# The scan's decay exponents: one GpSimd addition over four heads in place of four ScalarE activations with bias

## The chip, the core and the metric

The kernel runs on one core of a Trainium2 chip. The metric is the device time of one execution in microseconds (us), lower is better. The engines of the core are called as in the profile: PE is TensorE (matmuls; PEld its weight loads), DVE is VectorE, ACT is ScalarE, POOL is GpSimd, and SP is SyncE, which issues nearly all DMAs.

## The reference, cut to what matters

The reference is one layer of a bidirectional hybrid encoder: RMS norm, one input projection, three parallel groups (a chunked state-space scan, a windowed attention, an attention over a memory), gates, and an output projection with a residual. There are ten tiles of 128 tokens: eight of the sample, two of the prompt. The change lies in the scan, of which this is the part that counts:

```
acs = jnp.cumsum(dt * A.astype(f32).reshape(g, r), axis=2)
xdt = xs * dt[..., None]
seg = acs[:, :, :, None] - acs[:, :, None, :]
decay = jnp.exp(jnp.where(tril, seg, -jnp.inf))
cb = jnp.einsum('bcign,bcjgn->bcijg', Cm, Bm)
y_diag = jnp.einsum('bcijgr,bcjgrp->bcigrp', cb[..., None] * decay, xdt)
```

A chunk is a tile of 128 tokens, there are 16 heads and two directions. For each tile, direction and head the kernel needs a 128x128 matrix of exponents: the cumulated decay of position i (along a row) plus a value that belongs to position j (one per partition: the logarithm of the step less the cumulated decay).

## The kernel before, in words

TensorE works on large projections in blocks. A block streams weights of 128x512 from HBM (L209, L271: four buffers), splits each into a rounded part (ACT, L202) and the rest (DVE, L203), three buffers each, and multiplies the activations with both (L254 to L256 where tokens are the output's rows, L289 to L291 where features are). At the beginning and at the end, blocks in seven products are used (L1199 to L1201); there POOL makes sums of weights (L1171).

Beside the projections of the middle part run small generators: attention (`attn`, L583), memory attention (`mem_attn`, L704), preparation of keys (`k_prep`, L476), the scan upward (`ssd_up`, L798) and downward (`ssd_down`, L998). Each generator does a little and yields. Two lanes hold the queues of generators, and after each step of a block `pump` (L155) lets the lanes go on by rates that are written out by hand (RATES, L32). The framework then orders the instructions of each engine from this sequence, from priorities, and from what it reckons to be ready. Every engine and the SP queue work in their order: what waits holds up what stands behind it.

`ssd_up` treats a tile of 128 tokens in four quarters of four heads. For a quarter q:

- `rows(q)` (L836) loads two tiles of 128x512, rf for the forward and rb (called mt in the code) for the backward direction: for each of four heads 128 cumulated decays, the same on all partitions. rf has two buffers, rb three. So the load of a late quarter waits until an earlier quarter's tile has been read: rf by the selection (L919), rb by the products of `diag` (L931).
- `expo(q)` (L908) adds to each group of 128 columns the value of its head, one per partition, from `wj_all` (a column of it per head).
- `choose(q)` (L916) selects on DVE between the two directions by the triangle (L919) and takes the exponential on ACT (L920), in place in rb.
- `weights(q)` (L922) multiplies by the product of C and B on DVE (L924).
- `diag(g)` (L927) multiplies with the inputs of eight heads on TensorE (L931, into py) and adds the result up on DVE (L937).

At L940 to L974 these stand in this order: `expo(0)`, three yields, `choose(0)`, `expo(1)`, `rows(2)`, three yields, `weights(0)`, `choose(1)`, a yield, `expo(2)`, a yield, `weights(1)`, a yield, `diag(0)`, `choose(2)`, `rows(3)`, three yields, `weights(2)`, a yield, `expo(3)`, two yields, `choose(3)`, a yield, `weights(3)`, two yields, `diag(1)`.

POOL has little to do in this part: `rsqrt` (L119) computes one over a root for attention (qr), keys (krr), memory attention (mr) and the scan downward (yrs) in two instructions (L120, L121), and DVE uses the result (L604, L488, L742, L984).

`hv(r, 4)` sees 512 columns as four times 128; `hb(a, 4, P)` spreads four columns so that each stands for 128.

Of the kernel before, what the change touches and what calls it, by code (L numbers as in the profile page):

```python
# [15 lines left out]
AF = mybir.ActivationFunctionType  # L16
ALU = mybir.AluOpType
AX = mybir.AxisListType

P = 128  # L20
# [23 lines left out]
def hymba_encoder_kernel(  # L44
# [7 lines left out]
    V, A, G, T, S = nc.vector, nc.scalar, nc.gpsimd, nc.tensor, nc.sync  # L52
# [26 lines left out]
    def lconst(shape, name, dtype=F32):  # L79
        return cl.tile(shape, dtype, tag=name, name=name)  # L80
# [42 lines left out]
    def hv(ap, n=8):  # L123
        return ap.rearrange("p (h d) -> p h d", h=n)

    def hb(ap, n, d):
        return ap.unsqueeze(2).broadcast_to([P, n, d])
# [670 lines left out]
    def ssd_up(t):  # L798
# [30 lines left out]
        for g in range(2):  # L829
            c = slice(8 * g, 8 * g + 8)  # L830
            V.scalar_tensor_tensor(out=dco[:, c], in0=dt_all[:, t, 16 + 8 * g:24 + 8 * g], scalar=cbd[:, g:g + 1],
                                   in1=dskip[:, c], op0=ALU.mult, op1=ALU.add)
# [29 lines left out]
        for g in range(2):  # L862
            c = slice(g * 512, (g + 1) * 512)
# [44 lines left out]
        def expo(q):  # L908

            for d, r in enumerate(rows_[q]):  # L910
                for j in range(4):
                    c = slice(j * P, (j + 1) * P)
                    h = 16 * d + 4 * q + j
                    A.activation(r[:, c], r[:, c], AF.Identity, bias=wj_all[:, (t + 1) % 6, h:h + 1])

        def choose(q):  # L916

# [9 lines left out]
        def diag(g):  # L927
# [10 lines left out]
            S.dma_start(yp_d[t][:, g * 512:(g + 1) * 512], ya[g])  # L938

        expo(0)  # L940
        yield
        yield
        yield
        choose(0)
        expo(1)
        rows(2)
        yield
# [3 lines left out]
        choose(1)  # L951
        yield
        expo(2)
        yield
        weights(1)
# [557 lines left out]
    wj_all = lconst([P, 6, 32], "wj_all")  # L1513
# [167 lines left out]
```

## Time and profile before

| what | value |
|---|---|
| median of 3 runs | 1804.47 us (1803.84 to 1804.49) |
| span of the profiled execution, first to last instruction | 1800.7 us |
| median of the runs less this span | 3.77 us |
| instructions | 30423 |
| granted TensorE clock, mean | 1.000 |
| `expo` on ACT | 320 activations of 128x128, from 492.5 to 1452.6 us |
| selection on DVE (L919) | 40 of 128x512, 742 ns each |
| exponential on ACT (L920) | 40 of 128x512, 630 ns each |
| POOL additions of 128x128 (L1171) | 4 x 144, in the first and the last part only |

Of the profiled execution only the span is given, so times are set against it and the 3.77 us are carried along. The profile has a page (busy time of each engine, the chain of work that ended last, the costliest groups of instructions) and answers to questions: groups of instructions by line, who waited for whom, busy time in chosen stretches, the chain, and single instructions in order of time. A row such as `L914 ACT ACTIVATE rf<-rf,wj_all 128x128 f32<-128x128 f32 x160` names line, engine, operation, tiles and shape written and read, and the count. Durations of matmuls overlap and their ends are modelled.

### The profile page before, as it was taken

How to read it: one execution, taken by the hardware profiler on the slowest of the kernel's cores; microseconds unless marked ns; L12 is line 12 of the kernel's file. 1: busy time of each engine (PE TensorE's matmuls, PEld its weight loads, DVE VectorE, ACT ScalarE, POOL GpSimd, SP SyncE). 2: the span in 40 equal slices, each digit the busy share in tenths (PEclk: the TensorE clock that was granted, in tenths of full speed). 3: DMA queues.
4: the chain of work that ended last, by engine and by line, in shares of the span. 5: the costliest groups of instructions: out<-in, count | busy, mean ns of one | idle time of the engine just before them, and what ended most of it. 6: DMA issues, size and time to landing. Idle time of an engine off the chain costs nothing.

```text
span 1800.7 us, 30423 instructions
## 1 busy us (share of the span) xinstructions
PE 1791.2 (99%) x10546; PEld 1606.1 (89%) x10546; DVE 1244.3 (69%) x2422; ACT 903.0 (50%) x2039; POOL 439.5 (24%) x714
## 2 busy tenths in 40 slices
PE   9999999999999999999999999999999999999999
PEld 7789999999887899999989987887898888889999
DVE  5595788877657978775755866666885654866665
ACT  6554455444445756564435646544574533543332
POOL 0105789961110000000000000001100000058775
PEclk9999999999999999999999999999999999999999
DMA  8664455446544644444436355457785564644442
GB/s 291 198 179 120 138 153 146 129 136 218 164 136 147 184 134 140 121 132 134 119 96 192 110 161 180 128 178 235 231 266 168 184 190 138 216 153 147 142 143 80
DMA packets 198891, 290.58 MB, mean 161 GB/s; under 512 B 18960, under 2 KB 80464, under 8 KB 198736
## 3 DMA queue, kind: packets, MB, share of 16 engines
q1 hardware_dynamic: 198592, 288.57, 52.7%
q8 instruction: 83, 1.36, 0.3%
q14 instruction: 72, 0.59, 0.1%
q10 hardware_dynamic: 144, 0.06, 0.0%
HBM read 231.12 MB, written 57.44 MB: 160 GB/s over the span
## 4 chain that ended last, share of the span: by engine, by line
PE 61%; DVE 1%; ACT 1%; issue 1%; DMA 1%; POOL 0%; POOLq 0%; ACTq 0%; DVEq 0%
PE acc L254 9%; PE acc L256 8%; PE acc L255 8%; PE acc L289 5%; PE acc L291 5%; PE acc L290 5%; PE acc L1199 3%; PE acc L1201 3%; PE acc L1200 3%; PE py L931 2%; PE po L674 1%; PE ppt L664 1%; PE accm L1200 1%; PE accm L1201 1%; PE accm L1199 1%
## 5 line engine op out<-in xcount | busy, mean ns | idle before, releaser
L203 DVE TENSOR_TENSOR wl<-wraw,wh 128x512 fp32r<-128x512 f32 (+1 forms) x480 | 338.9, 708 | 241.3 <-ACT wh L202 230.7
L254 PE MATMUL acc<-wh,xH 128*128 128x512 f32 (+1 forms) x1248 | 481.9, 386 | 0.2 <-ACT mkr L416 0.2
L255 PE MATMUL acc<-wl,xH 128*128 128x512 f32 (+1 forms) x1248 | 472.2, 378 | 0.9 <-DVE wl L203 0.6
L256 PE MATMUL acc<-wh,xL 128*128 128x512 f32 (+1 forms) x1248 | 472.8, 379 | 0.0
L202 ACT ACTIVATE wh<-wraw 128x512 fp32r<-128x512 f32 (+1 forms) x480 | 292.4, 613 | 323.5 <-PE acc L256 173.3
L254 PEld LDWEIGHTS acc<-wh,xH 128*128 128x128 f32 x1248 | 234.5, 188 | 45.1 <-issue 4.8
L255 PEld LDWEIGHTS acc<-wl,xH 128*128 128x128 f32 x1248 | 234.7, 188 | 43.8 <-DVE wl L203 3.3
L256 PEld LDWEIGHTS acc<-wh,xL 128*128 128x128 f32 x1248 | 234.2, 188 | 43.9 <-issue 0.9
L289 PE MATMUL acc<-xH,wh 128*128 128x320 f32 x640 | 204.5, 320 | 0.0
L291 PE MATMUL acc<-xH,wl 128*128 128x320 f32 x640 | 198.6, 310 | 0.0
L290 PE MATMUL acc<-xL,wh 128*128 128x320 f32 x640 | 198.3, 310 | 0.0
L203 DVE TENSOR_TENSOR sl<-ws,sh 128x384 fp32r<-128x384 f32 x144 | 99.6, 695 | 96.9 <-ACT sh L202 96.6
L202 ACT ACTIVATE sh<-ws 128x384 fp32r<-128x384 f32 x144 | 74.6, 523 | 176.5 <-POOL ws L1171 81.5
L1171 POOL TENSOR_TENSOR ws<-wraw 128x128 f32<-128x128 f32 x144 | 91.1, 633 | 202.0 <-DMA wraw<-in_w_in_pairs_dram 83.6
L289 PEld LDWEIGHTS acc<-xH,wh 128*128 128x128 f32 x640 | 120.3, 188 | 4.1 <-issue 3.7
L290 PEld LDWEIGHTS acc<-xL,wh 128*128 128x128 f32 x640 | 120.3, 188 | 2.6 <-issue 2.2
L291 PEld LDWEIGHTS acc<-xH,wl 128*128 128x128 f32 x640 | 120.1, 188 | 0.7 <-issue 0.6
L1171 POOL TENSOR_TENSOR ws<-wraw,ws 128x128 f32<-128x128 f32 x144 | 93.5, 649 | 11.3
L358 DVE SCALAR_TENSOR_TENSOR c<-u,vec,c 128x638 f32<-128x638 f32 (+1 forms) x96 | 88.6, 926 | 10.0 <-ACT c L353 9.7
L1171 POOL TENSOR_TENSOR ws<-ws,wraw 128x128 f32<-128x128 f32 x144 | 94.2, 654 | 0.0
L120 POOL TENSOR_SCALAR qr<-qss 128x8 f32<-128x8 f32 x10 | 4.3, 428 | 366.6 <-DVE qss L598 366.6
L1171 POOL TENSOR_TENSOR wraw<-wraw 128x128 f32<-128x128 f32 x144 | 89.2, 620 | 11.1
(427 smaller groups left out, 3645.1 us busy)
## 6 DMA issues: line engine op xcount, KB each, us to landing
wraw<-in_w_in_laid_dram SPq DMA_DIRECT2D x208, 256.0 KB, 2.8
wraw<-in_w_in_pairs_dram SPq DMA_DIRECT2D x80, 256.0 KB, 2.8
wraw<-in_w_out_laid_dram SPq DMA_DIRECT2D x64, 256.0 KB, 3.5
wraw<-in_w_out_pairs_dram SPq DMA_DIRECT2D x64, 256.0 KB, 2.8
rf<-ac SPq DMA_DIRECT2D x40, 256.0 KB, 3.7
rb<-ac SPq DMA_DIRECT2D x40, 256.0 KB, 4.1
wraw<-in_w_mem_laid_dram SPq DMA_DIRECT2D x32, 256.0 KB, 4.8
xst<-in_x_sample_dram SPq DMA_DIRECT2D x20, 256.0 KB, 4.7
```

The costliest lines, as they stand in the source:

```text
L202: a = A.activation(h, raw, AF.Copy)
L203: b = V.tensor_sub(l, raw, h.bitcast(F32))
L254: T.matmul(ps[t][:, :n], sh, h[:, :n], start=(k_ == 0), stop=False)
L255: T.matmul(ps[t][:, :n], sh, l[:, :n], start=False, stop=False)
L256: T.matmul(ps[t][:, :n], sl, h[:, :n], start=False, stop=(k_ == KT - 1))
L289: T.matmul(o, sh, cur["H", q][:, m, c], start=(k == 0), stop=False)
L290: T.matmul(o, sh, cur["L", q][:, m, c], start=False, stop=False)
L291: T.matmul(o, sl, cur["H", q][:, m, c], start=False, stop=(k == KT - 1))
L358: V.scalar_tensor_tensor(out=c[0], in0=u[:, k:k + n], scalar=cw[k], in1=c[0], op0=ALU.mult, op1=ALU.add)
L1171: G.tensor_tensor(out=o, in0=x, in1=y, op=op)
L1199: T.matmul(ps[p], h, xh, start=(k_ == 0), stop=False)
L1200: T.matmul(ps[p], h, xl, start=False, stop=False)
```

## The change

In `expo`, the four activations per direction, each with 128 columns and a bias of one value per partition, become one addition on POOL over 512 columns, whose second operand is four columns of `wj_all`, each spread over 128.

```diff
         def expo(q):
 
             for d, r in enumerate(rows_[q]):
-                for j in range(4):
-                    c = slice(j * P, (j + 1) * P)
-                    h = 16 * d + 4 * q + j
-                    A.activation(r[:, c], r[:, c], AF.Identity, bias=wj_all[:, (t + 1) % 6, h:h + 1])
+                h = 16 * d + 4 * q
+                G.tensor_tensor(out=hv(r, 4), in0=hv(r, 4), in1=hb(wj_all[:, (t + 1) % 6, h:h + 4], 4, P), op=ALU.add)
```

Over the ten tiles 320 activations on ACT become 80 additions on POOL. Nothing else is edited.

## The prediction

> **What bounds the kernel now.** I read the page's busy shares first, then the chain that ended last, then the waits of TensorE in the stretch in which the ten scan tiles run, 490 to 1460 us.
>
> ```profile
> PE 1791.2 (99%) x10546; PEld 1606.1 (89%) x10546; DVE 1244.3 (69%) x2422; ACT 903.0 (50%) x2039; POOL 439.5 (24%) x714
> ...
> PE 61%; DVE 1%; ACT 1%; issue 1%; DMA 1%; POOL 0%; POOLq 0%; ACTq 0%; DVEq 0%
> ...
> 490.00:1460.00 970.00, 967.16 (x5695) 845.80 (x5694) 676.54 (x1479) 522.39 (x1308) 53.56 (x81) 1.00 0.53 162
> ```
>
> TensorE is busy for 1791.2 us of a span of 1800.7 us and has 61% of the chain; every other engine has 1% or less. In the scan stretch (the last line gives length, then busy us of PE, PEld, DVE, ACT and POOL, then the granted clock) it is busy for 967.2 of 970.0 us at a clock of 1.00, while ScalarE (ACT) works 522 us, VectorE (DVE) 677 and GpSimd (POOL) 54. The change touches no matmul. It can only shorten or lengthen the time in which TensorE waits for ACT and DVE, so those waits are the whole stake on the good side. Here they are, for the matmuls and then for the weight loads (line, releaser, total us, times, longest):
>
> ```profile
> PE pmt L759 <- DVE mpr L751: 1.3, 2, 0.8
> PE ppt L664 <- DVE lg L652: 0.9, 2, 0.5
> PE po L674 <- ACT so L995: 0.3, 1, 0.3
> PE psc L632 <- ACT qT L618: 0.2, 1, 0.2
> ```
>
> ```profile
> PEld psc L632 <- ACT pT L665: 1.7, 6, 0.5
> PEld psc L632 <- ACT qT L618: 1.5, 4, 0.6
> ...
> PEld pmt L759 <- ACT wh L202: 1.0, 1, 1.0
> ...
> PEld ppt L664 <- ACT wh L202: 0.8, 1, 0.8
> ...
> PEld pmt L759 <- ACT rb L920: 0.6, 1, 0.6
> ...
> PEld po L674 <- ACT so L995: 0.6, 1, 0.6
> PEld ppt L664 <- ACT pT L665: 0.6, 2, 0.3
> ```
>
> The matmul rows sum to 2.7 us, the weight-load rows that name ACT to 6.8 us (1.7 + 1.5 + 1.0 + 0.8 + 0.6 + 0.6 + 0.6). Together 9.5 us, and a part is counted twice or hidden under a running matmul. That is the ceiling of any gain: 0.5% of the time.
>
> **What the change removes.**
>
> ```profile
> L914 ACT ACTIVATE rf<-rf,wj_all 128x128 f32<-128x128 f32 x160 | 52.8, 392 | 2.7 <-DMA rf<-ac 2.7
> L914 ACT ACTIVATE rb<-rb,wj_all 128x128 f32<-128x128 f32 x160 | 52.5, 391 | 31.7 <-DMA rb<-ac 31.7
> ```
>
> From ACT go 320 activations, 52.8 + 52.5 = 105.3 us, and the 34.4 us (2.7 + 31.7) in which ACT stood still before them because the broadcast rows had not landed. Nearly all of that is one event per tile: the second tile (rb) of the fourth quarter is loaded only when the products of the first half (py) have released a buffer. One such event, as the chain of work shows it (start, length, what):
>
> ```profile
> 712.56 0.85 PE py L931 x8
> 713.42 3.68 DMA rb<-ac
> 717.19 0.40 ACT rb L914
> ...
> 718.10 0.79 ACT lg L647 x3
> 718.89 0.52 ACT wh L202
> 719.41 0.89 ACT rb L914 x3
> 720.32 0.73 DVE rb L919
> 721.05 0.31 DVE lg L652
> 721.41 0.88 PE ppt L664 x6
> ```
>
> The attention's exponentials (L647) and a weight rounding (L202) stand in ACT's queue behind an activation that waits for a DMA, and the transposes at 721.41 come late on TensorE. With the addition on POOL that queue runs on. What TensorE gets back: of the waits above, those that name a rounding or the decay's exponential (1.0 + 0.8 + 0.6 = 2.4 us) can be tied to this queue; qT, pT and so are followed from many places. I take **2.0 us off**; the ends are 0 (all of it hidden, or late for DVE next) and 9.5.
>
> **What it adds.** 80 additions of 128x512 on POOL, 53.6 us busy in 970 today. No such operation is in the trace; the nearest rows are POOL's additions of 128x128 and two selects, 128x128 and 128x384 wide (ns: least/median/most for the first two rows and the last two, a single one in the third):
>
> ```profile
> L1171 POOL TENSOR_TENSOR ws<-ws,wraw x144: 450/586/1044, 48.4 to 1783.8; 128x128 f32<-128x128 f32 x144
> L548 POOL TENSOR_SCALAR_AFFINE_SELECT lower<-one x2: 294/294/294, 431.2 to 864.8; 128x128 f32<-128x128 f32 x2
> L1430 POOL TENSOR_SCALAR_AFFINE_SELECT dist<-dist x1: 507/507/507, 424.6 to 424.6; 128x384 f32<-128x384 f32 x1
> L203 DVE TENSOR_TENSOR sl<-ws,sh x144: 542/722/868, 50.0 to 1787.4; 128x384 fp32r<-128x384 f32 x144
> ```
>
> The selects give 213 ns for 256 columns, 0.83 ns a column, so a fixed part of 294 - 107 = 187 ns. Taken off the least addition, 263 ns remain for 128 columns, 2.05 ns each, and 512 columns cost 187 + 1052 = **1.24 us**. Bounds: 0.45 (width costs nothing) and 4 x 0.586 = 2.34 us (nothing is fixed, and the addition waits as often as today's); I take 1.24, which uses the two rows that differ in width alone. The repeated column (one value along 128) is counted at nothing: bounded by the same 2.34. Two additions, 2.5 us, stand in place of two groups of four activations, of which one group reads so:
>
> ```profile
> 709.17 1.30 ACT L914 ACTIVATE rf<-rf,wj_all 128x128 f32<-128x128 f32 x4
> ```
>
> That is 1.30 us, 2.6 for two. So the decay's exponent is ready after its DMA as early as now, within 0.1 us, and earlier where ACT was the one that was late. POOL's total rises to 54 + 99 = 153 us of 970, far from a bound. The selection on DVE (L919) waits for POOL instead of ACT; behind it on DVE stand the weight differences (L203), as now. The SyncE queue is unchanged: the row loads wait for the selection (L919) and for py, neither of which moves by more than what is said here.
>
> The cost is on **DVE**. The last row above is a DVE subtraction that runs beside POOL's additions: 542 ns at least, 722 at the median, 868 at most. So DVE is held up by up to 326 ns beside an addition whose variable part is 263 ns: the whole of it, not a share. By that, a 512-wide addition holds a DVE operation for anything between 0 and 1.05 us, and 80 of them for 0 to 84 us; I take half, 0.53 each, 42 us in all, since operations of DVE that read one tile from SBUF or from PSUM need not meet it and a start in mid-addition waits for the rest alone. Where does that hurt? These are the stretches from a tile's first exponent to its last, with their sum; the second to sixth numbers as above:
>
> ```profile
> 579.00:635.00 56.00, 55.84 (x291) 44.58 (x291) 52.90 (x106) 41.23 (x103) 3.67 (x4) 1.00 0.67 198
> 674.00:725.00 51.00, 50.53 (x346) 47.41 (x344) 43.55 (x94) 33.84 (x88) 3.01 (x2) 1.00 0.47 141
> ...
> sum 448.00, PE 446.48 PEld 383.82 DVE 322.08 ACT 291.94 POOL 30.64; mean PE 44.65 PEld 38.38 DVE 32.21 ACT 29.19 POOL 3.06
> ```
>
> Over ten tiles DVE has 448 - 322 = 126 us idle, so 42 us fit. In the tile at 579 us they don't: DVE is idle for 3.1 of 56 us and eight additions ask for 4.2, so 1.1 us run over. Elsewhere the lead of the weights covers one delay of 0.5 us, which is read from ACT, whose roundings wait for TensorE to release a buffer:
>
> ```profile
> ACT wh L202 <- PE acc L256: 100.5, 50, 4.5
> ACT wh L202 <- PE acc L290: 37.0, 28, 2.9
> ```
>
> A mean of 100.5 / 50 = 2.0 us and 37.0 / 28 = 1.3 us. If that cover is gone, each delay counts in full on TensorE. I add **1.1 us**.
>
> **The sum.** Of the profiled execution the page gives the span, 1800.7 us; the median of the runs, 1804.47, lies 3.77 above. 1800.7 - 2.0 + 1.1 = 1799.8; with 3.77 it is 1803.6 us, 0.05% below the median. That is inside the 0.2% (3.6 us) which I take as what a measurement of this kernel can tell from no change.
>
> **The rivals.**
>
> B, *ACT's queue is behind all the ACT waits*: the qT and pT rows fall too, because ACT has 140 us less in its way. Then 6.8 go and 1.1 come: 1804.47 - 5.7 = 1798.8 us. For it: ACT is 65% busy in the ten stretches (291.9 of 448) and loses a third of that. Against: those waits are up to 0.6 us each, many small ones, and the attention chain alternates with DVE, which gets busier.
>
> C, *POOL's queue takes over the wait* (slower). The additions that wait for the late rb now stand in POOL's line, and behind them the pairs that compute a root for q, k and mq, for which DVE waits in its own line. The place, a row of POOL and one of ACT:
>
> ```profile
> 966.26 0.57 POOL L120 TENSOR_SCALAR qr<-qss 128x8 f32<-128x8 f32 x1 [14.23 <-DVE qss L598]
> ```
> ```profile
> 969.32 0.42 ACT L610 ACTIVATE qh<-q 128x256 fp32r<-128x256 f32 x1 [1.18 <-DVE q L604]
> ...
> 976.29 0.99 ACT L914 ACTIVATE rb<-rb,wj_all 128x128 f32<-128x128 f32 x3 [4.45 <-DMA rb<-ac]
> ```
>
> The q root starts at 966.26, the late rb lands at 976.29. Is the addition ahead of the root in POOL's order, the root is 10 us late, DVE stands at L604, and with a lead of 2.0 us TensorE loses 8 us: 1803.6 + 8 = 1811.6 us for one such case. It decides from the point where the addition precedes the root. Against: in ACT's order of before, work that needs the root (L610) stands ahead of the rb activations, so the order was laid out with the late row in mind.
>
> D, *DVE is held for every addition in full* (slower): 8 x 1.05 = 8.4 us per tile against 3.1 us of idle time in the stretch at 579 and 7.5 at 674. So 5.3 + 0.9 = 6.2 us run over in place of 1.1: 1803.6 + 5.1 = 1808.7 us. For it: the 326 ns of the DVE row above; against: its median is only 180 ns above the least.
>
> The Trainium skill's page "SBUF — State Buffer", section "Who interferes with whom", makes D a rule: GpSimd shares a port pair with VectorE, the pair is an exclusive lock, and a VectorE instruction with two SBUF inputs blocks entirely against a GpSimd instruction that reads SBUF. By that rule the sum would be D's; the trace agrees on the most that it shows (326 ns) and leaves open how often the two meet in the scan.
>
> E, *the addition is no faster than four narrow ones*, 2.34 us: a pair takes 4.7 us where ACT takes 2.6, and the late fourth quarter of ten tiles comes 2.1 us later; less the lead of 1.3 to 2.0 us, up to 0.8 x 10 = 8 us: 1811.6 us.
>
> **How the numbers follow.** Forecast 0.56, B 0.15, C 0.13, D 0.11, E 0.05. Faster by over 0.2% (under 1800.9) is B: 0.15. Slower by over 0.2% (over 1808.1) are C, D and E: 0.29. The rest, 0.56, is within. The likeliest case has its own range of 1801 to 1807; the range for 8 in 10 goes to B's 1798.5 below and to 1811 above, just short of one C or E.
>
> **What would show it.** The L914 rows gone from ACT, 80 additions on POOL near 1.24 to 1.6 us; ACT near 800 us busy; the rb wait of some 30 us listed under POOL; DVE's two-input operations in the stretches longer by a few tenths on average and by up to 1.05 us at most; TensorE's waits on ACT wh and rb gone and those on DVE wl or lg slightly up. A root on POOL that starts many us after its sum speaks for C, a mean addition above 2 us for E. The forecast is wrong if TensorE's waits in 490 to 1460 us change by more than 3.6 us either way, or if the order of the matmuls changes so that waits come up where there were none.

## The result, and the profile after

| kernel | median | runs | ratio to before (95% interval) | span of the profiled execution |
|---|---|---|---|---|
| before | 1804.15 us (1802.88 to 1804.49) | 4 | 1 | 1800.7 us |
| after | 1813.55 us (1812.26 to 1815.3) | 4 | 1.0056 (1.0042 to 1.0070) | 1810.8 us |

The kernel became slower by 9.4 us, where 0.9 us off was forecast. The profiled execution is longer by 10.1 us. Its page, with the span, the busy time of each engine and the shares of the chain that ended last:

```profile
span 1810.8 us, 30261 instructions
...
PE 1793.8 (99%) x10546; PEld 1607.3 (89%) x10546; DVE 1272.4 (70%) x2422; ACT 813.3 (45%) x1719; POOL 531.0 (29%) x794
...
PE 59%; DVE 3%; issue 2%; ACT 1%; DMA 1%; POOL 0%; POOLq 0%; SPq 0%; ACTq 0%; DVEq 0%
```

ACT went from 903.0 to 813.3 us and POOL from 439.5 to 531.0, as a plain exchange of work would have it. DVE executes the same 2422 instructions, yet is busy for 28.1 us more (1272.4 - 1244.3), and its share of the chain rose from 1% to 3%. The matmuls' waits in the stretch of the scan tiles (490 to 1480 us; line, releaser, total us, times, longest):

```profile
PE ppt L664 <- DVE lg L652: 2.9, 4, 1.5
PE pmt L759 <- DVE mpr L751: 2.8, 3, 1.7
PE pxs L850 <- ACT pT L665: 1.7, 1, 1.7
PE psc L632 <- DVE lg L634: 0.9, 1, 0.9
PE psc L632 <- ACT qT L618: 0.8, 1, 0.8
PE pms L739 <- DVE mql L724: 0.4, 1, 0.4
PE po L674 <- ACT so L993: 0.3, 1, 0.3
```

They sum to 9.8 us against 2.7 before, so 7.1 of the 10.1 us stand here, in a few stalls of up to 1.7 us. Where they come from is seen in the lengths of DVE's instructions. First the kernel before, then after (ns: least/median/most):

```profile
L649 DVE TENSOR_TENSOR den<-den,es x40: 147/160/163, 563.1 to 1346.3; 128x2 f32<-128x2 f32 x40
L652 DVE TENSOR_SCALAR lg<-lg,den x80: 343/412/435, 564.5 to 1348.8; 128x384 f32<-128x384 f32 x48, 128x256 f32<-128x256 f32 x32
L634 DVE SCALAR_TENSOR_TENSOR lg<-ndist,psc x80: 399/544/570, 558.5 to 1339.6; 128x384 f32<-128x384 bf16 x48, 128x256 f32<-128x256 bf16 x32
```

```profile
L649 DVE TENSOR_TENSOR den<-den,es x40: 144/155/999, 562.8 to 1355.1; 128x2 f32<-128x2 f32 x40
L652 DVE TENSOR_SCALAR lg<-lg,den x80: 336/409/1131, 564.2 to 1357.7; 128x384 f32<-128x384 f32 x48, 128x256 f32<-128x256 f32 x32
L634 DVE SCALAR_TENSOR_TENSOR lg<-ndist,psc x80: 400/540/555, 558.1 to 1349.0; 128x384 f32<-128x384 bf16 x48, 128x256 f32<-128x256 bf16 x32
```

The medians stay; the longest grow. The sum of the softmax's denominator (L649), two columns wide, took at most 163 ns and now up to 999. The scaling that the transposes wait for (L652) took at most 435 and now up to 1131. L634, which reads one operand from PSUM, isn't touched: seven of its eighty instructions run beside an addition, and none of them is longer than usual by more than 6 ns. The additions, by the list of their line in the kernel after:

```profile
L912 POOL TENSOR_TENSOR rf<-rf,wj_all x40: 1037/1042/1950, 471.8 to 1442.7; 128x512 f32<-128x512 f32 x40
L912 POOL TENSOR_TENSOR rb<-rb,wj_all x40: 1037/1042/1532, 475.5 to 1461.8; 128x512 f32<-128x512 f32 x40
```

One takes 1.04 us alone, and the longest excess of L649 (999 - 160 = 839 ns) fits inside one. How such an event becomes a stall can be read instruction by instruction. From the rows in order of time of the kernel after, first DVE and POOL, then PE (start, length, what; in brackets the idle time before it and what ended it):

```profile
799.94 1.39 DVE L751 TENSOR_SCALAR mpr<-mpr,mden 128x256 f32<-128x256 f32 x2
...
805.35 0.62 DVE L751 TENSOR_SCALAR mpr<-mpr,mden 128x256 f32<-128x256 f32 x2
```
```profile
799.20 1.72 POOL L912 TENSOR_TENSOR rf<-rf,wj_all 128x512 f32<-128x512 f32 x1 [8.38 <-DVE rb L922]
```
```profile
805.86 0.63 PE L759 MATMUL pmt<-identr,mpr 128*128 128x128 f32 x4 [1.72 <-DVE mpr L751]
```

The memory attention's scaling of two tiles (L751) lasts 1.39 us while the addition runs from 799.20 to 800.92; the next such pair of this kernel, at 805.35 with no addition beside it, lasts 0.62. What stands behind the first pair on DVE is late by the difference, 0.77 us, and PE stands for 1.72 us before the transposes that read the second pair. So the hold accounts for less than half of this stall directly, and these transposes stood for 0.44 us in the kernel before already. That is one reading; whether it is the cause was for experiments.

### The profile page after: what moved, and what is told of

The parts are those of the page before. It is cut to its first block, busy times and chain, and to the rows that moved or that the text cites. A ratio compares the mean times of both kernels' runs of the same rounds, so it can differ in the third digit from the quotient of the medians.

```text
span 1810.8 us, 30261 instructions
## 1 busy us (share of the span) xinstructions
PE 1793.8 (99%) x10546; PEld 1607.3 (89%) x10546; DVE 1272.4 (70%) x2422; ACT 813.3 (45%) x1719; POOL 531.0 (29%) x794
## 4 chain that ended last, share of the span: by engine, by line
PE 59%; DVE 3%; issue 2%; ACT 1%; DMA 1%; POOL 0%; POOLq 0%; SPq 0%; ACTq 0%; DVEq 0%
PE acc L254 9%; PE acc L256 8%; PE acc L255 8%; PE acc L289 4%; PE acc L291 4%; PE acc L290 4%; PE acc L1197 3%; PE acc L1199 3%; PE acc L1198 3%; PE py L929 2%; PE po L674 1%; PE ppt L664 1%; PE accm L1199 1%; PE accm L1198 1%; PE accm L1197 1%
## 5 line engine op out<-in xcount | busy, mean ns | idle before, releaser
L203 DVE TENSOR_TENSOR wl<-wraw,wh 128x512 fp32r<-128x512 f32 (+1 forms) x480 | 348.7, 728 | 230.6 <-ACT wh L202 224.4
L255 PEld LDWEIGHTS acc<-wl,xH 128*128 128x128 f32 x1248 | 234.6, 188 | 44.6 <-DVE wl L203 3.7
L912 POOL TENSOR_TENSOR rf<-rf,wj_all 128x512 f32<-128x512 f32 x40 | 48.4, 1211 | 273.4 <-DMA rf<-ac 173.3
L358 DVE SCALAR_TENSOR_TENSOR c<-u,vec,c 128x638 f32<-128x638 f32 (+1 forms) x96 | 92.4, 966 | 9.1 <-ACT c L353 8.7
```

Source lines behind the costliest of these rows:

```text
L203: b = V.tensor_sub(l, raw, h.bitcast(F32))
L255: T.matmul(ps[t][:, :n], sh, l[:, :n], start=False, stop=False)
L358: V.scalar_tensor_tensor(out=c[0], in0=u[:, k:k + n], scalar=cw[k], in1=c[0], op0=ALU.mult, op1=ALU.add)
```

## The experiments

**Theory 1, holds.** A POOL instruction that reads SBUF keeps certain DVE instructions waiting until it has ended. The attention's small ones are held for far longer than they last, PE runs out of work for a moment, and the loss has nothing to do with which instruction waits for which. **Theory 2, order and late wait.** The additions give results at other times and in another order: DVE's selection waits for POOL, the late rb row now holds something else up, and the instructions of PE and DVE are laid out anew.

**No addition at all.** The loops are left empty; this tells what a relieved ACT, the changed order and the late rows bring without any work on POOL.

```diff
-                for j in range(4):
-                    ...
+                continue
```

> Leaves out the addition of the column values altogether (the selection reads the loaded rows as they are): ACT loses the 320 activations, POOL gets nothing. Theory 1 (POOL's additions hold DVE, which shares its way into SBUF with POOL): without additions nothing is held, so the time is that of before or up to 4 us less, and DVE busy stays near 1244 us. Theory 2 (the order: the selection and the exponential stand at the head of the DVE and ACT queues and wait there for the late row, whoever adds): 3 to 8 us above before, as in the changed kernel, with TensorE waits on the attention's DVE results.

Measured: 1.0010 (1.0001 to 1.0019), span 1802.4 us. Its page and two of the matmuls' waits:

```profile
PE 1791.8 (99%) x10546; PEld 1606.5 (89%) x10546; DVE 1245.6 (69%) x2422; ACT 814.4 (45%) x1719; POOL 439.2 (24%) x714
```
```profile
PE ppt L664 <- DVE xs L852: 1.9, 1, 1.9
PE pmt L759 <- DVE mpr L751: 0.8, 2, 0.5
```

ACT has 88.6 us less to do and no gain shows. Theory 1 had allowed for up to 4 us less, theory 2 for 3 to 8 us more; 0.1% more came, at the edge of the interval. PE executes its 10546 matmuls in the same order as in the kernel after, and the transposes that ended the stall of 1.72 us there wait for 0.31 us here:

```profile
801.16 0.63 PE L759 MATMUL pmt<-identr,mpr 128*128 128x128 f32 x4 [0.31 <-DVE mpr L751]
```

So the new order by itself costs some 0.1%, and the rest of the 0.56% comes with the additions on POOL, by holds or by their late results.

**Half of the change.** Only the forward rows, or only the backward rows, go to POOL; the other direction stays on ACT.

```diff
+                if d == 0:
+                    h = 16 * d + 4 * q
+                    G.tensor_tensor(out=hv(r, 4), in0=hv(r, 4), in1=hb(wj_all[:, (t + 1) % 6, h:h + 4], 4, P), op=ALU.add)
+                    continue
                 for j in range(4):
```

> Only the forward row (rf) is added on POOL, 40 additions; the backward row (rb), the one that lands late, stays with ACT. Theory 1: half of the additions, so half of the loss, 3 to 6 us above before, DVE busy up by about 14 us. Theory 2: the late wait stays where it was, so within 1 us of before.

> Only the backward row (rb) is added on POOL, 40 additions, with its late load; rf stays with ACT. Theory 1: half of the loss, 3 to 6 us above before, DVE busy up by about 14 us. Theory 2: all of the loss, 8 to 10 us.

Measured: forward (d == 0) 1.0034 (1.0021 to 1.0046), backward (d == 1) 1.0015 (1.0007 to 1.0024). The pages, forward first:

```profile
PE 1790.8 (99%) x10546; PEld 1605.7 (89%) x10546; DVE 1263.3 (70%) x2422; ACT 857.9 (47%) x1879; POOL 488.6 (27%) x754
```
```profile
PE 1790.5 (99%) x10546; PEld 1606.2 (89%) x10546; DVE 1255.2 (70%) x2422; ACT 858.2 (48%) x1879; POOL 483.9 (27%) x754
```

The forward half loses 0.34%, 6.1 us, at the upper end of what theory 1 gave (3 to 6 us) and not within the 1 us of theory 2. The backward half loses 0.15%, 2.7 us, below what either theory gave and hardly above the 0.10% without any addition. The two together lose 0.49%, near the 0.56 of the whole. DVE's extra busy time adds up as well: 19.0 + 10.9 = 29.9 us against 28.1. The forward half costs more, although the late row that the order theory blames is the backward one.

**The kernel before, with additions that nobody waits for.** After its own activations, `expo` of before issues on POOL two additions of the change's form into a buffer whose content isn't used, in eight of the ten tiles (64 in all).

```diff
+            if t >= 2:
+                for _ in range(2):
+                    G.tensor_tensor(out=hv(rbc[:, :512], 4), in0=hv(rbc[:, :512], 4), in1=hb(rows_[q][0][:, 0:4], 4, P), op=ALU.add)
```

> The kernel before with all its ACT activations, and beside them 64 extra POOL additions of 128x512 (tiles 2 to 9) on a tile that nobody reads afterwards, started by the forward row. Nothing on DVE or ACT waits for them. Theory 1: 64 of 80 additions, so 5 to 9 us above before and DVE busy up by some 20 us. Theory 2: no wait is moved, so within 1 us of before.

Measured: 1.0096 (1.0081 to 1.0112), some 17 us, more than the change itself and twice the 5 to 9 us that theory 1 gave. All of ACT's work is as before, no instruction of another engine waits for the additions, and PE and DVE execute their instructions in the very order of before. From the page, DVE is busier by 25.5 us:

```profile
PE 1796.5 (99%) x10546; PEld 1610.7 (89%) x10546; DVE 1269.8 (70%) x2422; ACT 903.0 (50%) x2039; POOL 518.1 (29%) x778
```

Its largest stall in order of time, with the same two steps of the downward pass (L358) in the kernel before in the first fence:

```profile
709.51 1.69 DVE L358 SCALAR_TENSOR_TENSOR c<-u,vec,c 128x646 f32<-128x646 f32 x2
```
```profile
711.29 3.25 DVE L358 SCALAR_TENSOR_TENSOR c<-u,vec,c 128x646 f32<-128x646 f32 x2
```
```profile
710.98 2.87 POOL L917 TENSOR_TENSOR rbc<-rbc,rf 128x512 f32<-128x512 f32 x2 [12.36 <-ACT rf L914]
```
```profile
715.05 0.44 PE L632 MATMUL psc<-kT,qT 128*128 128x384 f32 x1 [4.13 <-DVE lg L634]
```

Two operations of 1.69 us last 3.25 beside two additions of 2.87 us together, and PE, which waits for the next operation of DVE, stands for 4.13 us. The hold of 1.56 us is a part of that; DVE also comes to the pair 1.78 us later than before. In this execution, 12.1 us longer than before, the waits of PE between 490 and 1490 us rise from 2.7 to 10.0 us, and the clock is at half for 10.2 us (last section), which costs about 5.1 more. Additions that serve nobody are enough for a loss, as theory 1 says; theory 2 gave less than 1 us.

**The same POOL time without reading.** Four fills of 512 columns with zero in place of the two additions (and one small copy, which was to tie them to the same moment).

```diff
+            if t >= 2:
+                G.tensor_copy(out=rbc[:, 600:601], in_=rows_[q][0][:, 0:1])
+                for _ in range(4):
+                    G.memset(rbc[:, :512], 0.0)
```

> The kernel before with all its ACT activations; beside them in tiles 2 to 9, after a one-column copy that ties them to the forward row, four POOL memsets of 512 columns per quarter on a tile that nobody reads afterwards, about 2 us of POOL time per quarter as in the run with the extra additions, but without reading SBUF. Theory 1 in its narrow form (what is held is DVE's second read, by POOL's reading): within 2 us of before, and DVE operations with two inputs in SBUF keep their length. In its wide form (any POOL work holds DVE): 8 to 17 us above before.

Measured: 1.0008 (1.0000 to 1.0017). From its page, and the fills by the list of their line:

```profile
PE 1791.9 (99%) x10546; PEld 1606.6 (89%) x10546; DVE 1249.2 (69%) x2422; ACT 902.3 (50%) x2039; POOL 516.2 (29%) x874
```
```profile
L918 POOL MEMSET rbc<- x128: 522/527/687, 640.4 to 718.4; 128x512 f32 x128
```

POOL is as busy as with the additions (516.2 and 518.1 us), and the loss is 0.08% in place of 0.96. But the times can't be compared like for like: the copy did not tie the fills, and all 128 run one after the other between 640 and 718 us, where the 64 additions lie between 673 and 1459. What the run does show is what happens to DVE's instructions beside 68 us of fills. Two lines of the kernel with unused additions, then the same two with fills:

```profile
L358 DVE SCALAR_TENSOR_TENSOR c<-u,vec,c x96: 867/884/1666, 200.2 to 917.4; 128x638 f32<-128x638 f32 x48, 128x646 f32<-128x646 f32 x48
...
L652 DVE TENSOR_SCALAR lg<-lg,den x80: 340/410/1195, 562.5 to 1360.4; 128x384 f32<-128x384 f32 x48, 128x256 f32<-128x256 f32 x32
```
```profile
L358 DVE SCALAR_TENSOR_TENSOR c<-u,vec,c x96: 868/886/1161, 202.5 to 909.1; 128x638 f32<-128x638 f32 x48, 128x646 f32<-128x646 f32 x48
...
L652 DVE TENSOR_SCALAR lg<-lg,den x80: 341/412/792, 563.6 to 1350.2; 128x384 f32<-128x384 f32 x48, 128x256 f32<-128x256 f32 x32
```

Beside fills, the instruction with two tiles from SBUF (L358) isn't held: its most, 1161 ns, is that of the kernel before (1160), and the 14 of its instructions that meet a fill are within 14 ns of their usual length. The scaling of one tile (L652) is held, all eight that meet a fill, by 240 to 377 ns. By the Trainium skill's page "SBUF — State Buffer", section "Who interferes with whom", an instruction with two SBUF inputs meets POOL's reads and not its writes, and a `tensor_scalar` in a two-port mode meets both. The trace agrees with both halves: 1666 and 1161 ns for L358, 1195 and 792 for L652; that L652 runs in such a mode is not shown by any row.

**Shorter holds.** The addition cut into four of 128 columns.

```diff
-                    A.activation(r[:, c], r[:, c], AF.Identity, bias=wj_all[:, (t + 1) % 6, h:h + 1])
+                    G.tensor_tensor(out=r[:, c], in0=r[:, c], in1=wj_all[:, (t + 1) % 6, h:h + 1].broadcast_to([P, P]), op=ALU.add)
```

> The changed kernel with each POOL addition cut into four of 128 columns, 320 in all; by today's rows 0.45 us each alone, so 1.8 us for a tile of 512 in place of 1.2. Theory 1a (a DVE instruction is held to the end of the POOL instruction that it meets, so long instructions hurt): shorter holds, at most 0.3 us, DVE busy up by less than the 28 us of the changed kernel or about the same, time 3 to 8 us above before. Theory 1b (only the sum of POOL's time counts): more POOL time, so 10 to 15 us above before.

Measured: 1.0041 (1.0029 to 1.0054), span 1808.1 us. L649 by the list of its line:

```profile
L649 DVE TENSOR_TENSOR den<-den,es x40: 143/159/379, 562.4 to 1352.9; 128x2 f32<-128x2 f32 x40
```

The longest L649 falls from 999 to 379 ns and DVE's extra busy time from 28.1 to 15.7 us (1260.0), while POOL is busy for longer (597.4 against 531.0 us). The ratio lies below that of the whole addition, but the intervals overlap: that shorter holds cost less is shown for DVE, and for the total only likely.

**One operand as a scalar.** The form with a value per partition, again in four pieces, so that POOL reads only one tile.

```diff
-                    A.activation(r[:, c], r[:, c], AF.Identity, bias=wj_all[:, (t + 1) % 6, h:h + 1])
+                    G.tensor_scalar(out=r[:, c], in0=r[:, c], scalar1=wj_all[:, (t + 1) % 6, h:h + 1], scalar2=None, op0=ALU.add)
```

> The changed kernel with 320 POOL operations of 128 columns that read one tile and one value per partition, in place of an addition of two tiles. By the selects of one input (294 ns for 128 columns, 0.83 ns a column) POOL reads for 0.42 us per tile of 512 where the addition reads for 1.05. Theory 1: the hold goes with the time in which POOL reads SBUF, so some 40 per cent of it: DVE busy up by 8 to 15 us, time 2 to 6 us above before. Theory 2 (order and late row): 1 to 2 us above before, as without any addition. If the operation costs as much as the addition of 128 columns, it comes out like split4.

Measured: 1.0062 (1.0049 to 1.0075), as slow as the change and above the 2 to 6 us of theory 1. My estimate of its length was wrong. The list of its line, and the waits of DVE's selection and of the transposes:

```profile
L914 POOL TENSOR_SCALAR rf<-rf,wj_all x160: 596/604/1771, 472.3 to 1447.0; 128x128 f32<-128x128 f32 x160
```
```profile
DVE rb L919 <- POOL rb L914: 33.5, 10, 6.0
```
```profile
PE ppt L664 <- DVE lg L652: 4.3, 2, 2.6
```

One piece takes 0.60 us at least, eight of them (a pair) 4.8, where ACT took 2.6. DVE's busy time rises by only 6.5 us (1250.8), but its selection now waits 33.5 us for POOL, and what stands behind it on DVE comes late for PE. This run loses by another way, the late result, which is the mechanism of rival E; it says nothing against theory 1, and it shows that holds aren't the only way to lose 0.6% here.

**The same addition on DVE.** Same count, same shape, another engine; the diff is against the kernel after.

```diff
-                G.tensor_tensor(out=hv(r, 4), in0=hv(r, 4), in1=hb(wj_all[:, (t + 1) % 6, h:h + 4], 4, P), op=ALU.add)
+                V.tensor_tensor(out=hv(r, 4), in0=hv(r, 4), in1=hb(wj_all[:, (t + 1) % 6, h:h + 4], 4, P), op=ALU.add)
```

> The same 80 additions of 128x512 on DVE, none on POOL, none on ACT. DVE gets 80 x 0.69 = 55 us of its own work, twice what the holds cost it in the changed kernel. Theory 1a (the holds hurt because they fall on small operations of the attention's chain, at any moment): the work stands in order just ahead of the selection and interrupts nothing, so no worse than the changed kernel, 2 to 9 us above before. Theory 1b (DVE time as such): twice the loss, 15 to 20 us above before.

Measured: 1.0006 (0.9997 to 1.0015), no difference from before and below the 2 to 9 us of theory 1a. The list of its line:

```profile
L912 DVE TENSOR_TENSOR rf<-rf,wj_all x40: 671/683/699, 493.7 to 1448.3; 128x512 f32<-128x512 f32 x40
L912 DVE TENSOR_TENSOR rb<-rb,wj_all x40: 675/686/694, 494.3 to 1454.1; 128x512 f32<-128x512 f32 x40
```

40 x 0.683 + 40 x 0.686 = 54.8 us of additional work in DVE's own line. DVE's busy time, in which overlapping ends count once, rises by 45.2 us (1289.5), 1.6 times the 28.1 us that the holds took, and it cost nothing that can be measured. So the idle time of DVE is real and can be used, and how much time DVE loses isn't what hurts. The reading that fits: DVE can stand 0.68 us at a time in its own order, and it can't, a few times in a run, when an operation on which PE waits is held by an engine that knows nothing of it.

No version was faster than the kernel before.

## Why the prediction was wrong, point by point

**What bounds the kernel: right.** PE is busy 99%, and 7.1 of the 10.1 us are time in which it waits. The ceiling of 9.5 us held for a gain alone, which the text said.

**The gain of 2.0 us: wrong, it is nothing.** Without the additions on any engine the ratio is 1.0010 (1.0001 to 1.0019). The waits on ACT that were to go came back one step further on. The exponential (L920, after the change L918) stands in the same queue and waits for the selection; first before, then after:

```profile
ACT rb L920 <- DVE rb L919: 20.1, 18, 3.1
```
```profile
ACT rb L918 <- DVE rb L917: 60.4, 27, 6.2
```

The weight loads show the same; first their two rows of after that name it:

```profile
PEld ppt L664 <- ACT rb L918: 1.9, 1, 1.9
PEld pmt L759 <- ACT rb L918: 0.8, 1, 0.8
...
PEld pmt L759 <- ACT wh L202: 0.6, 1, 0.6
```

With the rounding's row that is 3.3 us, where the rows wh and rb named 2.4 before. Without any addition, ACT's wait before the exponential is 44.4 us. An instruction that waits at the head of ACT's line was replaced by its successor, which waits for the same late row. Rival B falls with this term.

**The addition's length: right in size.** 1.24 us were taken; it is 1.04 alone, and on average 1.21 for rf and 1.12 for rb in the run (48.4 and 44.6 us in 40 each). The text's claim that the exponent is ready as early as before held too: DVE's selection waits 17.1 us in 7 waits for POOL where it waited 14.8 in 7 for ACT.

**The holds on DVE: the mechanism right, the conversion into time wrong. This is the step that failed.** The prediction took 42 us of holds, compared them with 126 us of idle time over ten tiles ("so 42 us fit") and let 1.1 us run over. The holds were fewer, 28.1 us, and the loss was 9.4. Idle time per tile is no cover for a hold: PE asks for an operation of DVE at a definite moment, and idle time earlier or later in the tile is of no use then. The lead of the weights, read from ACT's waits for PE (1.3 to 2.0 us), is not the lead of the attention's transposes. In the kernel before, instruction by instruction, the transposes begin less than 1.05 us after the scaling that they read has ended in 38 of 80 cases for L652 and in 14 of 40 for L751, and less than 0.5 us after it in 25 and 10. Their waits of 0.5 (L664) and 0.8 us (L759) at most before are 1.5 and 1.7 after. What settles it: 45.2 us more of plain work on DVE cost nothing (1.0006), and 25.5 us of holds from a POOL that serves nobody cost some 17 us (1.0096), a part of it by the clock.

**The granted clock: not in the sum.** In the kernel after, the clock fell to half behind one of the stalls. The windows (length, then busy us of PE, PEld, DVE, ACT and POOL, the granted clock, DMA share, GB/s):

```profile
1333.80:1335.80 2.00, 0.30 (x3) 0.04 (x1) 1.28 (x5) 2.00 (x8) 1.04 (x1) 1.00 1.00 391
1337.20:1340.60 3.40, 3.40 (x15) 3.40 (x14) 2.87 (x7) 2.10 (x4) 1.16 (x1) 0.51 0.65 217
1341.30:1345.00 3.70, 3.70 (x30) 3.69 (x29) 3.20 (x6) 2.21 (x5) 0.00 (x0) 1.00 0.61 185
```

In the second line PE is fully busy and yet does 15 matmuls in 3.4 us, in the third 30 in 3.7. Half of 3.4 is 1.7 us lost. With the 7.1 us of waits that makes 8.8 of the 10.1; the remaining 1.3 us I can't place.

**Rival C: did not come.** A root on POOL starts at most 2.2 us after its sum, once, instead of the 10 us that C needs; the root at 966 us, its place in the text, starts 0.09 us after. **Rival E** isn't the change's case (1.04 us, not 2.34), but the scalar form is just that, and in place of its price of 8 us came 11.2 (0.62% of 1802.85). **Rival D** was the right mechanism at the wrong place: it let the holds overflow the idle time of two tiles, for 1808.7 us. In truth they hit short operations of the attention all over the scan. The rule cited for D, from the Trainium skill's page "SBUF — State Buffer", section "Who interferes with whom", gave the right sign; I discounted it by a median that stays low beside POOL's additions, where the longest value was what counted.

**What would show it.** The rows gone from ACT, 80 additions, ACT near 800 us (813.3) came. So did DVE's two-input operations longer by up to 1.05 us at most, L649 by 0.84, and the bound given for a wrong forecast, over 3.6 us more of PE waits (7.1). The waits on wh and rb did not go.

**What stays open.** How the 0.46% between the kernel without additions and the changed one divides into holds and late results. At 629.62 us the transposes wait 1.47 us and DVE itself had waited 2.01 us at L917 for POOL's rb: that stall is a late row and no hold. Three others (720, 799 and 1331 us) are holds by the rows beside them.

## What to carry to other kernels

Before work is moved to GpSimd, look at the most, not the median, of VectorE's instruction lengths beside GpSimd instructions that read SBUF, and ask which of them TensorE waits for; compare a hold with the lead of that one consumer and not with idle time summed over a stage. Work in VectorE's own line can be free where the same work on GpSimd is not: try the engine that would be held first. If the engine relieved was not on the path that sets the end, price its relief at nothing until a version without the work shows otherwise.

## What the runs showed of the hardware that was not expected

**A stall costs more than its own length.** In all ten profiles the half clock shows in the scan for 3.4 us once in the kernel after (from 1337.1 us) and once in the scalar form (from 630.9), and in the kernel with unused additions for 6.8 us from 715.6 and 3.4 from 807.6; elsewhere, before included, never. It came after stalls of 1.71, 2.61, 4.13 and 2.29 us. It did not come after others of the same executions that were as long, so the length doesn't decide alone. The matmuls that ended a stall, with the stall in brackets, first in the kernel after, then in the scalar form:

```profile
629.62 0.84 PE L664 MATMUL ppt<-identr,lg 128*128 128x128 f32 x6 [1.47 <-DVE lg L652]
...
805.86 0.63 PE L759 MATMUL pmt<-identr,mpr 128*128 128x128 f32 x4 [1.72 <-DVE mpr L751]
...
1335.81 0.54 PE L850 MATMUL pxs<-identr,xc 128*128 128x128 f32 x4 [1.71 <-ACT pT L665]
```
```profile
630.99 1.30 PE L664 MATMUL ppt<-identr,lg 128*128 128x128 f32 x5 [2.61 <-DVE lg L652]
...
727.15 0.91 PE L664 MATMUL ppt<-identr,lg 128*128 128x128 f32 x6 [1.71 <-DVE lg L652]
...
1386.50 0.63 PE L759 MATMUL pmt<-identr,mpr 128*128 128x128 f32 x4 [2.28 <-DVE mpr L751]
```

Only 1335.81 and 630.99 are at a fall. The two falls of the kernel with unused additions lie 92.2 us apart, 27 times 3.41. The Trainium skill's page "TensorE: Matmul & The Clock Gate", section "What's actually happening", has a free-running window of 3413 ns and calls one idle window the condition. By an estimate from that figure, a raster laid through the fall of the same execution cuts the 1.72 us at 805.86 into 0.5 and 1.2, the 1.71 at 727.15 into 1.1 and 0.6 and the 2.28 at 1386.50 into two parts of at most 1.3, while each stall before a fall has at least 1.7 us, half a window, within one; the 1.47 at 629.62 lies whole in one window and is below half. The stretches of 3.4 us agree with the page; that the window must be wholly idle doesn't, since 1.71 us sufficed. Nor is half a window the whole rule. The forward half of the change has this stall:

```profile
803.23 0.63 PE L759 MATMUL pmt<-identr,mpr 128*128 128x128 f32 x4 [1.84 <-ACT mpT L763]
```

By the same estimate, with the raster laid through the clock's fall at the end of that execution, 1.8 of the 1.84 us lie in one window, and the clock stayed at 1.00. What more is needed stays open, as does why the clock was low for two windows after the longest stall; no run was made to test it.

**The scalar form is the slower one on GpSimd.** 128 columns with a value per partition take 0.60 us at least; the two-operand addition of 128 columns takes 0.39 at least (the run with shorter holds), that of 512 columns 1.04.
